# DeltaNet's 32-block forward substitution on VectorE instead of GpSimd

## The chip, the core and the metric

One core of one Trainium2 chip runs the whole program. The metric is device time in microseconds (us) for one execution. The engines are named as in the profile: PE (TensorE, matrix products), DVE (VectorE), ACT (ScalarE), POOL (GpSimd) and SP (SyncE, which issues most DMAs). Each takes its instructions in the order in which they stand in its own queue, and waits at the head of it until what the instruction needs is there.

## What is computed

The program is one decoder layer over 256 tokens of width 2048 in fp32: an input projection, three token mixers side by side (gated DeltaNet, Mamba-2 SSD, GLA), a merge, an MLP and a gated embedding. The change touches DeltaNet alone. Its reference, cut:

```python
m = jnp.where(strict, jnp.einsum('bnhik,bnhjk->bnhij', kb, k) * decay, 0.0)
a = m + jnp.eye(chunk, dtype=m.dtype)
u = lax.linalg.triangular_solve(a, v * beta[..., None], left_side=True, lower=True, unit_diagonal=True)
w = lax.linalg.triangular_solve(a, kb * jnp.exp(g)[..., None], left_side=True, lower=True, unit_diagonal=True)
```

The kernel works with chunks of 128 tokens, and solves with an explicit inverse T of the unit lower triangular matrix `a`. T is built from 32x32 diagonal blocks, each inverted by forward substitution; products on PE then join them to blocks of 64 and of 128.

## The kernel before

**Weights.** `weights` (L287 to L302) brings two k-tiles of a weight matrix at a time: one DMA from SP into a `raw` tile (512 KB for 512 columns, 344 KB for 344), a cast on ACT (L300) into `hi`, and a subtraction on DVE (L301, on record as L170, the line of the helper `tt`) into `lo`. PE then makes three products of each pair (hi with hi, lo with hi, hi with lo). There are four buffers each of `raw`, `hi` and `lo`. A fifth `hi` waits until PE has done with the first, a fifth `raw` until DVE has split the first. In what follows "the split lo_2263" is the subtraction that writes that tile; a chunk is the work of PE on one such tile.

**Mixers as background tasks.** The mixers run as generators (`Task`, `spawn`, `background`) between the projection's matmuls. A clock kept by the program, not by the chip, decides when a task goes a step further; a scheduler that knows priorities then puts the rows of each engine's queue in order. `feat_conv` makes a feature block of a mixer: products, DVE's copy out of PSUM (L170, with `r0bc`), twelve multiply-adds of a short convolution on DVE (L173, 128x256 each), a Silu on ACT (L457), and transposes on PE (L123) for whoever needs tokens on the partitions.

**DeltaNet.** `dn_task` runs twice, for four heads each (g = 0, 1: "group 0" and "group 1"). It makes M for two chunks of tokens, writes it to DRAM (L661), and reads it back with one 32x32 block for each of 32 partitions (L668). The 31 steps of the loop (L673 to L680) do the forward substitution there: step j multiplies a column of M with the rows of X that are done, and subtracts the product (two instructions, 31 to 256 elements on each partition, 5456 elements over the 31 steps for each of the two). L681 copies X transposed into XT. POOL then issues the DMAs that write both to DRAM (L682, L683), and four more that read them into tiles of 128 partitions, T and its transpose for either chunk of tokens (L688). PE's first use of T are 32x32 products, whose results ACT copies (L701) for the next products; ACT writes those into T (L716, L718), and stages of 64 and of 128 follow. The loop has the priority -LATER: in a queue it stands behind what else is ready.

Of the kernel before, what the change touches and what calls it, by code (L numbers as in the profile page):

```python
# [52 lines left out]
def tile_hybrid_block(ctx: ExitStack, tc: tile.TileContext, *args):  # L53
# [49 lines left out]
    def r3(ap, b):  # L103
        return ap.rearrange("p (a b) -> p a b", b=b)

    V, A, G = nc.vector, nc.scalar, nc.gpsimd
# [62 lines left out]
    def tt(eng, o, i0, i1, op):  # L169
        eng.tensor_tensor(out=o, in0=i0, in1=i1, op=op)  # L170
# [383 lines left out]
    def dr_blocks(d):  # L554
        return bass.AP(tensor=d.tensor, offset=d.offset, ap=[[HB // 4, 32], [P, 32], [1, 32]])
# [47 lines left out]
    def h4(tl):  # L603
        return lambda h: tl[:, h * P:(h + 1) * P]

    INV = G
    LATER = 1500

    def dn_task(g, qT, kT, vT):
# [63 lines left out]
        with tc.high_priority(-LATER):  # L673
            for j in range(31):
                n = 31 - j
                tmp = XT.rearrange("p a b -> p (a b)")[:, :n * (j + 1)]
                tmp = r3(tmp, j + 1)
                tt(INV, tmp, mb[:, j, j + 1:].unsqueeze(2).broadcast_to([32, n, j + 1]),
                   X[:, j, :j + 1].unsqueeze(1).broadcast_to([32, n, j + 1]), ALU.mult)
                tt(INV, X[:, j + 1:, :j + 1], X[:, j + 1:, :j + 1], tmp, ALU.subtract)  # L680
        INV.tensor_copy(out=XT, in_=X.rearrange("p i j -> p j i"))  # L681
        G.dma_start(out=dr_blocks(t_dr[0]), in_=X)  # L682
# [589 lines left out]
```

## Time and profile before

| | |
|---|---|
| runs shown | 1881.85, 1887.17, 1887.25 us (median 1887.17) |
| profiled execution | 1882.98 us |
| its span, first to last instruction | 1881.2 us |
| PE busy | 1846.9 us (98%) |
| DVE busy | 1161.0 us (62%) |
| POOL busy | 183.7 us (10%) |
| PE's granted clock, mean | 0.993 of full speed |
| the loop on POOL, group 0 | from 176.65 us, copy done at 230.74 |
| the loop on POOL, group 1 | from 313.66 us, copy done at 366.53 |

An engine's busy share is a mean over the span. Which engine is waited for at one place is read from what stands in brackets behind an instruction of the timeline: how long its engine idled before it, and what ended that.

### The profile page before, as it was taken

Reading aid. Unit: us, or ns where it says so; the run is one execution under the profiler, and the core shown is the slowest. Engines: PE = TensorE matmul, PEld = TensorE weight load, DVE = VectorE, ACT = ScalarE, POOL = GpSimd, SP = SyncE. Lnnn points to the kernel's source line nnn. Section 1 sums busy time; section 2 is a strip of 40 time slices with the busy share of each in tenths; the row PEclk is TensorE's granted clock in tenths of the full one; section 3 lists DMA queues with packets and bytes.
Section 4 is the critical chain, followed back from the end, with each engine's and each line's share of the span. In section 5 each row is a group of like instructions: output and inputs, shape, how many; then the busy total and the mean of one; then the engine's idle time right before and its main releaser. Section 6 shows DMA issues by size and latency. Waiting matters only on the chain.

```text
span 1881.2 us, 28343 instructions
## 1 busy us (share of the span) xinstructions
PE 1846.9 (98%) x11256; PEld 1659.0 (88%) x11256; DVE 1161.0 (62%) x1518; ACT 934.9 (50%) x1200; POOL 183.7 (10%) x243
## 2 busy tenths in 40 slices
PE   8999999899999999999999999999999999999997
PEld 8999989899888788888888898899889988998886
DVE  6567947878566666554565755455555555555675
ACT  6745564576455564454444644444433443444664
POOL 0004814800201220000000000000000000000001
PEclk9999989999999999999999999999999999999999
DMA  7765565465665546667676565666566566656563
GB/s 250 218 184 175 147 186 165 137 182 145 196 201 168 172 143 192 195 183 196 186 246 204 175 185 190 191 189 181 191 192 188 180 192 195 184 182 195 183 207 129
DMA packets 185573, 348.07 MB, mean 185 GB/s; under 512 B 14296, under 2 KB 33103, under 8 KB 184544
## 3 DMA queue, kind: packets, MB, share of 16 engines
q1 hardware_dynamic: 182992, 334.69, 58.8%
q0 software_dynamic: 2416, 11.56, 1.8%
q8 instruction: 88, 1.44, 0.3%
q14 instruction: 45, 0.37, 0.1%
q10 hardware_dynamic: 32, 0.01, 0.0%
HBM read 340.41 MB, written 5.80 MB: 184 GB/s over the span
## 4 chain that ended last, share of the span: by engine, by line
PE 69%; ACT 1%; POOL 1%; DVE 1%; issue 0%; DMA 0%; DVEq 0%; ACTq 0%
PE mm L114 67%; PE br L114 1%; PE br L123 1%; POOL b L170 1%; DVE lo L170 0%; ACT hi L300 0%; DMA raw<-in_w_in_dram 0%; DVE b L173 0%; ACT b L946 0%; ACT L1226 0%; ACT b L945 0%; ACT b L1114 0%; ACT L1236 0%; ACT b L1224 0%; DVE s L173 0%
## 5 line engine op out<-in xcount | busy, mean ns | idle before, releaser
L170 DVE TENSOR_TENSOR lo<-raw,hi 128x1024 fp32r<-128x1024 f32 (+2 forms) x644 | 771.7, 1202 | 621.9 <-ACT hi L300 618.5
L300 ACT CAST hi<-raw 128x1024 fp32r<-128x1024 f32 (+2 forms) x644 | 653.6, 1019 | 807.3 <-PE mm L114 702.3
L114 PE MATMUL mm<-ahi,hi 128*128 128x256 f32 x1728 | 492.2, 285 | 0.0
L114 PE MATMUL mm<-ahi,lo 128*128 128x256 f32 x1728 | 490.8, 284 | 0.0
L114 PE MATMUL mm<-alo,hi 128*128 128x256 f32 x1728 | 490.8, 284 | 0.0
L114 PE MATMUL mm<-hi,ahi 128*128 128x512 f32 (+2 forms) x992 | 372.0, 375 | 0.0
L114 PE MATMUL mm<-lo,ahi 128*128 128x512 f32 (+2 forms) x992 | 369.0, 372 | 2.8 <-DVE lo L170 1.6
L114 PE MATMUL mm<-hi,alo 128*128 128x512 f32 (+2 forms) x992 | 367.6, 371 | 0.0
L114 PEld LDWEIGHTS mm<-ahi,hi 128*128 128x128 f32 x1728 | 333.3, 193 | 0.5 <-ACT ahi L180 0.2
L114 PEld LDWEIGHTS mm<-alo,hi 128*128 128x128 f32 x1728 | 332.8, 193 | 0.8 <-issue 0.8
L114 PEld LDWEIGHTS mm<-ahi,lo 128*128 128x128 f32 x1728 | 333.3, 193 | 0.1
L114 PE MATMUL mm<-hi,m 128*128 128x512 f32 x1024 | 316.0, 389 | 0.0
L114 PEld LDWEIGHTS mm<-hi,m 128*128 128x128 f32 x1024 | 192.2, 188 | 39.9
L114 PEld LDWEIGHTS mm<-lo,ahi 128*128 128x128 f32 x992 | 187.2, 189 | 32.3 <-DVE lo L170 4.0
L114 PEld LDWEIGHTS mm<-hi,ahi 128*128 128x128 f32 x992 | 187.1, 189 | 28.0 <-issue 0.2
L114 PEld LDWEIGHTS mm<-hi,alo 128*128 128x128 f32 x992 | 187.1, 189 | 27.5
L114 PE MATMUL mm<-lo,m 128*128 128x512 f32 x512 | 199.2, 389 | 0.0
L114 PE MATMUL mm<-hi,b 128*128 128x512 f32 x416 | 134.1, 393 | 0.7 <-ACT hi L300 0.7
L114 PEld LDWEIGHTS mm<-lo,m 128*128 128x128 f32 x512 | 96.1, 188 | 19.7
L170 POOL TENSOR_TENSOR b<-b 128x128 f32<-128x128 f32 (+16 forms) x118 | 78.4, 679 | 162.0 <-ACT b L939 149.9
L114 PEld LDWEIGHTS mm<-hi,b 128*128 128x128 f32 x416 | 78.1, 188 | 17.0 <-ACT hi L300 1.1
L114 PE MATMUL mm<-lo,b 128*128 128x512 f32 x208 | 81.3, 391 | 0.8 <-DVE lo L170 0.8
(257 smaller groups left out, 1130.0 us busy)
## 6 DMA issues: line engine op xcount, KB each, us to landing
raw<-in_w_in_dram SPq DMA_DIRECT2D x200, 512.0 KB, 4.1
raw<-in_w_up_dram SPq DMA_DIRECT2D x128, 512.0 KB, 3.8
raw<-in_w_down_dram SPq DMA_DIRECT2D x128, 512.0 KB, 3.8
raw<-in_w_branch_dram SPq DMA_DIRECT2D x48, 512.0 KB, 4.6
raw<-in_w_in_dram SPq DMA_DIRECT2D x48, 344.0 KB, 3.5
raw<-in_w_out_dram SPq DMA_DIRECT2D x32, 512.0 KB, 4.8
raw<-in_w_ple_gate_dram SPq DMA_DIRECT2D x32, 512.0 KB, 4.5
raw<-in_w_in_dram SPq DMA_DIRECT2D x16, 352.0 KB, 3.4
```

Source lines behind the costliest of these rows:

```text
L114: nc.tensor.matmul(o, lhsT=lhsT, rhs=rhs, start=start, stop=stop, **kw)
L123: nc.tensor.transpose(o, i, ident)
L170: eng.tensor_tensor(out=o, in0=i0, in1=i1, op=op)
L300: A.copy(out=hi[:, :, :n], in_=raw[:, :, :n])
```

## The change

One name changes: the two tensor_tensor instructions of the loop and the copy L681 go to VectorE. Data, shapes, priority, and the DMAs that POOL issues stay.

```diff
-    INV = G
+    INV = V
     LATER = 1500
...
                 tt(INV, tmp, mb[:, j, j + 1:].unsqueeze(2).broadcast_to([32, n, j + 1]),
                    X[:, j, :j + 1].unsqueeze(1).broadcast_to([32, n, j + 1]), ALU.mult)
                 tt(INV, X[:, j + 1:, :j + 1], X[:, j + 1:, :j + 1], tmp, ALU.subtract)
         INV.tensor_copy(out=XT, in_=X.rearrange("p i j -> p j i"))
```

The scheduler puts the rows anew. DVE's queue has 62 instructions and a copy more for each group. Those of group 0 stand between the splits lo_2209 and lo_2820, those of group 1 between lo_3787 and lo_5033. This is the difference on DVE at the start of group 0; b_284 is X with M, b_285 the product:

```order
 L170 TENSOR_TENSOR lo_2209<-raw_2207,hi_2208 128x1024
+L170 TENSOR_TENSOR b_285_1942<-b_284_1941 32x31
+L170 TENSOR_TENSOR b_284_1941<-b_284_1941,b_285_1942 32x31
 L170 TENSOR_TENSOR lo_2263<-raw_2261,hi_2262 128x1024
+L170 TENSOR_TENSOR b_285_1942<-b_284_1941 32x60
+L170 TENSOR_TENSOR b_284_1941<-b_284_1941,b_285_1942 32x30x2
+L170 TENSOR_TENSOR b_285_1942<-b_284_1941 32x87
+L170 TENSOR_TENSOR b_284_1941<-b_284_1941,b_285_1942 32x29x3
+L170 TENSOR_TENSOR b_285_1942<-b_284_1941 32x112
+L170 TENSOR_TENSOR b_284_1941<-b_284_1941,b_285_1942 32x28x4
+L170 TENSOR_TENSOR b_285_1942<-b_284_1941 32x135
 L170 TENSOR_TENSOR lo_2293<-raw_2291,hi_2292 128x1024
```

Up to seven of them now stand between two splits. PE's queue is the same in the whole of group 0. In group 1 the copy stands as follows on DVE (b_515 is X, b_516 XT and then T):

```order
+L170 TENSOR_TENSOR b_516_3508<-b_515_3507 32x31
+L170 TENSOR_TENSOR b_515_3507<-b_515_3507,b_516_3508 32x31
 L170 TENSOR_TENSOR lo_5015<-raw_5013,hi_5014 128x2x344
+L681 COPY b_516_3508<-b_515_3507 32x1024
 L170 TENSOR_TENSOR lo_5033<-raw_5031,hi_5032 128x2x344
```

Before, POOL had made that copy at 366.53 us; the split that now stands behind it, lo_5033, ran at 406.28 us. PE's first products with group 1's T moved back by seven chunks, from the chunk of hi_4831 to that of hi_5068, where they now stand close to the products that need their results (b_686, b_687). PE's queue there, after:

```order
 L114 MATMUL mm_4879<-lo_5069,ahi_86 128x344
+L114 MATMUL br_4603<-b_516_3508,b_465_3206 32x32 x4
+L114 MATMUL br_4614<-b_516_3508,b_467_3214 32x32 x4
+L114 MATMUL br_4625<-c_651_4448,c_646_4427 128x64 x3
+L114 MATMUL br_4603<-b_516_3508,b_465_3206 32x32 x4
+L114 MATMUL br_4614<-b_516_3508,b_467_3214 32x32 x4
+L114 MATMUL br_4625<-c_651_4448,c_646_4427 128x64
+L114 MATMUL br_4625<-c_651_4448,c_648_4435 128x64 x4
+L114 MATMUL br_4637<-c_655_4457,bn_4455 128x512
+L114 MATMUL br_4669<-b_516_3508,b_686_4601 32x32 x4
```

Before, four chunks lay between br_4614 and br_4669. On ACT the copies L701 that lie between the two have also moved, behind two casts for the next projection, hi_5111 and hi_5141:

```order
+L300 CAST hi_5111<-raw_5110 128x1024
+L300 CAST hi_5141<-raw_5140 128x1024
+L701 COPY b_686_4601<-br_4603 32x128
+L701 COPY b_687_4602<-br_4614 32x128
+L701 COPY b_686_4601<-br_4603 32x128
+L701 COPY b_687_4602<-br_4614 32x128
```

Behind these places the queues meet the old order again; the last row of PE that differs belongs to group 1's final products, some 330 rows further on.

## Rows read from the trace of the kernel before

**Rows 1.** The page: busy time, share of the span, instructions.
```profile
PE 1846.9 (98%) x11256; PEld 1659.0 (88%) x11256; DVE 1161.0 (62%) x1518; ACT 934.9 (50%) x1200; POOL 183.7 (10%) x243
```

**Rows 2.** Busy us (instructions) by engine in three stretches, granted clock, DMA share.
```profile
120.00:177.00 57.00, 57.00 (x482) 57.00 (x481) 42.35 (x72) 28.03 (x35) 9.25 (x9) 1.00 0.61 178
177.00:231.00 54.00, 52.96 (x392) 52.38 (x391) 46.42 (x54) 28.58 (x42) 49.24 (x63) 1.00 0.55 153
...
314.00:367.00 53.00, 47.53 (x373) 46.80 (x372) 40.48 (x49) 25.29 (x34) 48.18 (x63) 0.97 0.47 135
```

**Rows 3.** Timeline of POOL: start, us, engine, line, op; the loop's ends.
```profile
176.65 0.23 POOL L170 TENSOR_TENSOR b<-b 32x31 f32<-32x31 f32 x1 [3.97 <-DMA b<-m_dr]
...
228.64 2.10 POOL L681 COPY b<-b 32x1024 f32<-32x1024 f32 x1
...
234.41 0.79 POOL L688 DMA_DIRECT2D b<-t_dr  x1 [2.13 <-DMA t_dr<-b]
```

**Rows 4.** Groups of DVE's instructions, 120 to 177 us: busy, mean ns.
```profile
L170 DVE TENSOR_TENSOR lo<-raw,hi 128x1024 fp32r<-128x1024 f32 x18 | 22.6, 1255 | 15.0 <-ACT hi L300 14.8
L173 DVE SCALAR_TENSOR_TENSOR b<-b,rowT,b 128x256 f32<-128x256 f32 x24 | 10.2, 479 | 0.0
...
L170 DVE TENSOR_TENSOR b<-br,s 128x512 f32<-128x512 f32 x3 | 2.0, 681 | 0.0
```

**Rows 5.** The same, 177 to 231 us, while POOL runs the loop.
```profile
L173 DVE SCALAR_TENSOR_TENSOR b<-b,rowT,b 128x256 f32<-128x256 f32 x24 | 17.6, 777 | 0.6 <-ACT b L452 0.6
L170 DVE TENSOR_TENSOR lo<-raw,hi 128x1024 fp32r<-128x1024 f32 x7 | 10.1, 1442 | 4.1 <-ACT hi L300 4.1
L170 DVE TENSOR_TENSOR lo<-raw,hi 128x704 fp32r<-128x704 f32 x8 | 9.9, 1246 | 0.6 <-ACT hi L300 0.6
...
L271 DVE TENSOR_SCALAR s<-s 128x32 f32<-128x32 f32 x1 | 1.9, 1948 | 0.7 <-ACT s L270 0.7
```

**Rows 6.** The same, 314 to 367 us, while POOL runs group 1's loop.
```profile
L173 DVE SCALAR_TENSOR_TENSOR b<-b,rowT,b 128x256 f32<-128x256 f32 x19 | 14.7, 813 | 0.1
...
L170 DVE TENSOR_TENSOR cbm<-br,cst 128x128 f32<-128x128 f32 x2 | 0.6, 284 | 1.2 <-PE br L114 1.2
```

**Rows 7.** Timeline of DVE: two short instructions, each needing the one before.
```profile
292.88 0.17 DVE L170 TENSOR_TENSOR s<-s 128x8 f32<-128x8 f32 x1
293.08 0.37 DVE L173 SCALAR_TENSOR_TENSOR s<-s,s 128x8 f32<-128x8 f32 x2
```

**Rows 8.** Groups of DVE's instructions, whole span: one that reads with a stride.
```profile
L968 DVE TENSOR_REDUCE ga<-c 128x128 f32<-128x512 f32 x8 | 8.4, 1056 | 0.0
```

**Rows 9.** PE's waits, 165 to 525 us: us, times, longest.
```profile
PE br L123 <- ACT b L457: 5.5, 1, 5.5
...
PE mm L114 <- DVE b L437: 0.9, 1, 0.9
```

**Rows 10.** Timeline of PE at the first products with group 0's T.
```profile
242.21 0.69 PE L114 MATMUL br<-b,b 32*32 32x32 f32 x16
...
243.57 0.32 PE L114 MATMUL mm<-lo,ahi 128*128 128x344 f32 x1
243.72 0.32 PE L114 MATMUL mm<-hi,alo 128*128 128x344 f32 x1
246.66 0.53 PE L114 MATMUL br<-b,b 32*32 32x32 f32 x6 [2.62 <-ACT b L701]
```

**Rows 11.** DMA issues of 225 to 260 us: KB each, us to landing.
```profile
b<-t_dr POOLq DMA_DIRECT2D x4, 256.0 KB, 6.5
```

**Rows 12.** Timeline of ACT before PE's wait at 345 us.
```profile
343.87 1.06 ACT L457 ACTIVATE b<-b 128x1024 f32<-128x1024 f32 x1 [5.39 <-DVE b L173]
```

**Rows 13.** Stretches after PE's waits: busy us by engine, granted clock.
```profile
246.00:256.00 10.00, 9.34 (x76) 7.73 (x77) 2.53 (x6) 5.07 (x13) 0.00 (x0) 0.51 0.70 193
346.00:348.00 2.00, 2.00 (x11) 2.00 (x11) 1.44 (x4) 0.85 (x2) 1.84 (x3) 0.51 0.67 175
```

**Rows 14.** Timeline of PE at the first products with group 1's T.
```profile
398.73 0.69 PE L114 MATMUL br<-b,b 32*32 32x32 f32 x16
```

## Prediction

> **What bounds the kernel now.** The page's first part says that PE is busy for 1846.9 us, 98% of the span [rows 1]. So the end moves only when PE waits less or more, or runs at another clock. The next view is the table of windows: POOL's loops fill the stretches 177 to 231 and 314 to 367 us, and PE has 1.0 us of idle time in the first and 5.5 in the second [rows 2]. That 5.5 us is all that the profile offers for removal while the loop runs. POOL itself is not waited for there: its loop of group 0 runs from 176.65 us to 230.74 (the copy's end) [rows 3], that of group 1 ends at 366.53, and PE's first products with T come at 242.21 [rows 10] and 398.73 us [rows 14]. The change can then act in three ways: POOL's quiet may speed up DVE, DVE's added work may make splits late for PE, and T may come too late.
>
> **What DVE gets rid of.** The groups of DVE's instructions in the stretch before the loop, compared with the same groups during it, show the price of POOL's company. A multiply-add of the convolutions (128x256) takes 479 ns while POOL is nearly quiet [rows 4], 777 ns in group 0's loop [rows 5], and 813 in group 1's [rows 6]. A 1024-wide split takes 1255 against 1442 ns.
>
> The Trainium skill (page "SBUF — State Buffer", section "Who interferes with whom") says that DVE's second pair of SBUF ports is shared with GpSimd, as an exclusive lock. The trace agrees for instructions with two SBUF operands (479 against 777 ns), and by that rule a quiet POOL would give the difference back.
>
> In group 0 the excess is 24 x 0.298 = 7.2 us for the multiply-adds, 7 x 0.187 = 1.3 for the wide splits, 8 x 0.36 = 2.9 for the 704-wide splits (1246 ns against 0.88 by the line below), and 1.8 for L271, together 13.2 us. In group 1 the multiply-adds alone have 19 x 0.334 = 6.3 us.
>
> **What DVE gets.** A tensor_tensor takes 284 ns for 128 elements [rows 6] and 681 for 512, one of whose operands is broadcast as in the loop [rows 4]; the line through them is 0.15 us + 1.04 ns for an element. The loop is a chain, each instruction needing the one before; such a pair stands at 292.88 + 0.17 = 293.05 and 293.08 us, a gap of 0.03 to 0.04 [rows 7]. So one costs 0.186 us + 1.04 ns an element: 62 x 0.186 = 11.5, plus 10912 x 1.04 ns = 11.35, together 22.9 us. The copy reads with a stride of 32 words. If that is free it costs 0.15 + 1.07 = 1.2 us; if it is like the strided read of L968 (512 elements in 1056 ns, 1.77 ns each [rows 8]) it costs 2.0. I take 1.9, since the stride is what the two share. That makes 24.8 us a group, against 54.1 on POOL. A price of 1.77 ns for every element of the loop is the upper bound: 10912 x 0.73 ns = 8 us more.
>
> [...]
>
> **Group 0.** DVE is busy for 46.4 of 54 us [rows 2]. With the change that is 46.4 - 13.2 + 24.8 = 58.0 us from about 176.6 on, if it never idles: the copy ends at 233.4 (laid out row by row in the new order, where neighbours overlap by some hundredths) to 234.6. I take 233.7, that is 3 us later than POOL's. T then takes its old way: 3.7 us from the copy's end to the first read's issue (234.41 [rows 3]) and 6.5 us for a read [rows 11], that is 240.9 before, for a use at 242.21. The slack is 1.3 us, so PE waits about 1.7 us more. POOL's other rows here are memsets and the DMA L529, which now stands among T's reads instead of behind them, so it is issued about when it was. Splits: a late one made PE wait 0.9 us before (it is put down to L437, the row behind it) [rows 9]; laying out the new queue gives waits of 0.2, 0.6 and 1.0 us at lo_2762, lo_2780 and lo_2820, some 0.9 more, in which T comes nearer too, since PE is later for it. I put group 0 at +1.5 us, with bounds of -2 and +10 (the latter with the 8 us above).
>
> **Group 1, the start.** Here lies PE's longest wait, 5.5 us for the Silu of L457 [rows 9]. ACT idled 5.39 us before that Silu, until DVE's last multiply-add [rows 12]. Twelve of them precede it; without POOL each takes 0.334 us less, 4.0 us together, of which 0.3 goes to an instruction of the loop that now stands between them: 3.7 us less wait. The clock: after the wait it was granted at 0.51 in 346 to 348 us, the lower level of 1.2 GHz [rows 13], while the stretch with the wait of 0.9 us kept 1.00 [rows 2, 9]. If the wait shrinks to 1.7 us most of that half speed goes too, 1.2 us (of 2 to 3 us at half). Sum -4.9, between 0 and -7. Some two thirds of the loop's 24.8 us, 17 us, stand in the stretch up to 367 us, where DVE has 53 - 40.5 = 12.5 us idle [rows 2] and gets 6.3 back: it fits, just. The rest stands behind, up to 400 us; there PE reads a split some us after it is made, and none is late in my layout.
>
> **Group 1, the end.** The copy ends at about 398 us by the layout (before: 366.53). By the same 3.7 and 6.5 us T lands at about 408. PE's first products with it were at 398.73 us [rows 14]; they are now seven chunks later, each of 12 products at 0.155 us [rows 10], and the start's gain is taken off: 398.7 + 13 - 4.9 = 406.8. So the first of the four reads may be there in time, and the last has no slack. The products that follow need ACT's copies L701, which now stand behind hi_5141 and so behind a raw DMA that runs together with T's reads. In group 0 the same pattern made PE wait 2.62 us [rows 10], and the clock from 246 to 256 us had a mean of 0.51 [rows 13]. In the new place some 4 us of other small products lie between; I take +1 us, between 0 and +6.
>
> **Sum.** +1.5 - 4.9 + 1.0 = -2.4 us. The profiled execution took 1882.98 us (span 1881.2 and 1.8 around it), so 1880.6 us. It lies 4.2 us below the median of the runs shown and near the fastest; runs of one kernel differ by 5 us here, and 0.3% (5.6 us) is about what a measurement tells from no change.
>
> **The rivals.**
> *A larger gain.* The move of T's reads by 3 us may take them off the raw DMA that held ACT in group 0. Then the wait of 2.62 us [rows 10] and most of the 10 us near half clock [rows 13], some 3.5 of at most 5 us of PE's time, go as well, and group 1's new wait does not come: -2.4 - 1 - 2.6 - 3.5 = -9.5, 1873.5 us. For it: POOL's whole disturbance ends. Against it: T's reads and the weight reads still meet, only later.
> *A wait in a new place.* Group 1's T or its L701 comes late as in group 0: PE waits 2.6 us or more and loses 3.5 at half clock: -2.4 - 1 + 6 = +2.6, 1885.6 us. For it: the new order on ACT. Against it: the small products between.
> *DVE becomes the bound (slower).* The loop's operands, rows of 1 to 31 elements on 32 partitions, cost 1.77 ns an element. Then group 0's copy ends at 242 us and T comes 8 us later still, and in group 1 the copy ends some 6 us later, against no slack: -2.4 + 8 + 6 = +11.6, 1894.6 us, and more with half clock. The point from which it decides is about 1.3 ns an element (2.8 us more in each group). Against it: the broadcast operand in rows 4 runs at 1.04 ns.
> *The contention stays.* If something other than POOL slows DVE in these stretches, DVE has 46.4 + 24.8 = 71 us of work in 54, T is 17 us late in group 0, and it is 1897 us or more. Against it: the stretch before has the same instructions at 479 ns.
>
> **How the numbers follow.** The forecast has 0.42 (own range 1877 to 1884), the larger gain 0.28, the wait in a new place 0.17, DVE as the bound 0.09, the contention 0.04. Faster by over 0.3% holds most of the larger gain (0.25) and the forecast's lower edge (0.05): 0.30. Slower holds the last two and a quarter of the new wait: 0.17; the rest, 0.53, is within 0.3%. The range leaves out the end of the larger gain and of the last two: 1870 to 1893.
>
> **What would show it.** Right: the multiply-adds at 0.48 us in both stretches; the loop's 256-element instructions at about 0.42 us; group 0's copy at 1.9 us, ending near 233.7; PE's wait for L457 at 1 to 2.5 us; half clock gone after it. Wrong: multiply-adds still near 0.8; loop instructions above 0.5; PE's waits for splits beyond 3 us in 177 to 235; waits at T's first products beyond 4 us; group 1's L701 at the head of PE's waits.

## The result, and the profile after

The changed kernel took 1868.6 us (median of 4 executions, 1867.83 to 1870.28), beside 1884.5 us for the kernel before: a ratio of 0.9919, with a 95% interval from 0.9903 to 0.9936. In two later comparisons on other occasions the same kernel gave 0.9932 [0.9914, 0.9950] and 0.9939 [0.9919, 0.9958]. By these ratios the gain is some 11 to 15 us (the medians of the three comparisons lie 15.9, 11.5 and 8.8 us apart). The forecast was 2.4 us.

The profiled execution took 1870.28 us, 12.7 less than that of before. The page's busy times and two rows of the windows (busy us by engine, then granted clock and DMA share) answer to [rows 1, 2]:

```profile
PE 1840.2 (98%) x11256; PEld 1653.3 (88%) x11256; DVE 1172.0 (63%) x1644; ACT 930.6 (50%) x1197; POOL 88.8 (5%) x117
```

```profile
177.00:231.00 54.00, 54.00 (x404) 54.00 (x403) 51.81 (x121) 28.81 (x42) 0.00 (x0) 1.00 0.58 157
314.00:367.00 53.00, 52.55 (x409) 51.77 (x408) 51.12 (x109) 29.44 (x40) 0.00 (x0) 1.00 0.54 153
```

POOL is quiet in both stretches, DVE is busy for 51.8 of 54 and 51.1 of 53 us, and PE's idle time falls from 1.0 to nothing and from 5.5 to 0.45 us. The groups of DVE's instructions in the first stretch (busy us, mean ns) answer to [rows 4, 5]:

```profile
L173 DVE SCALAR_TENSOR_TENSOR b<-b,rowT,b 128x256 f32<-128x256 f32 x24 | 10.2, 467 | 0.0
L170 DVE TENSOR_TENSOR lo<-raw,hi 128x1024 fp32r<-128x1024 f32 x8 | 9.6, 1206 | 0.0
L170 DVE TENSOR_TENSOR lo<-raw,hi 128x704 fp32r<-128x704 f32 x8 | 7.0, 873 | 0.0
```

The multiply-adds are at 467 ns, where they had 777. The wide split is at 1206 ns: the 1255 of [rows 4], which I had taken for the quiet price, still had some of POOL's company in it (one of its 18 took 1.79 us, while POOL worked at 150 to 156 us). DVE's timeline shows the loop and the copy (start, us):

```profile
204.98 0.41 DVE L170 TENSOR_TENSOR b<-b 32x255 f32<-32x255 f32 x1
205.43 0.41 DVE L170 TENSOR_TENSOR b<-b,b 32x255 f32<-32x255 f32 x1
...
231.09 1.00 DVE L681 COPY b<-b 32x1024 f32<-32x1024 f32 x1
```

An instruction of 255 elements takes 0.41 us and the next starts 0.45 us after it, as forecast (0.186 + 255 x 1.04 ns = 0.45). The copy takes 1.00 us (1.17 in group 1), not 1.9. PE's waits from 165 to 525 us, the start of its products with group 0's T, and the Silu before group 1's transposes answer to [rows 9, 10, 12]:

```profile
PE br L114 <- DVE b L170: 1.8, 1, 1.8
PE br L114 <- ACT b L718: 1.7, 1, 1.7
...
PE br L114 <- DMA b<-t_dr: 0.5, 1, 0.5
PE br L123 <- ACT b L457: 0.5, 1, 0.5
```

```profile
243.25 0.66 PE L114 MATMUL br<-b,b 32*32 32x32 f32 x16 [0.52 <-DMA b<-t_dr]
...
244.98 0.43 PE L114 MATMUL br<-b,b 32*32 32x32 f32 x8
...
251.46 0.43 PE L114 MATMUL br<-b,b 32*32 32x32 f32 x8 [1.74 <-ACT b L718]
```

```profile
335.26 1.06 ACT L457 ACTIVATE b<-b 128x1024 f32<-128x1024 f32 x1 [0.60 <-DVE b L173]
```

The wait of 5.5 us for L457 is down to 0.5, and ACT idles 0.60 us before that Silu instead of 5.39. The wait of 2.62 us for L701 is gone; a new one of 1.74 us for L718 stands a stage further on. The clock, in windows that answer to [rows 13], with one more at group 1's products with T:

```profile
246.00:256.00 10.00, 8.26 (x95) 7.31 (x92) 4.28 (x11) 4.73 (x13) 0.00 (x0) 0.91 0.70 221
346.00:348.00 2.00, 2.00 (x19) 2.00 (x19) 1.90 (x5) 0.78 (x1) 0.00 (x0) 1.00 0.67 179
400.00:414.00 14.00, 14.00 (x158) 12.34 (x157) 9.80 (x11) 10.09 (x19) 0.00 (x0) 1.00 0.48 160
```

The stretch from 246 to 256 us has a clock of 0.91, where it had 0.51; what is left of the lower level there begins at 254 us, behind the wait for L718:

```profile
254.00:258.00 4.00, 4.00 (x23) 3.63 (x22) 1.04 (x5) 0.96 (x2) 0.00 (x0) 0.57 0.80 248
```

Adding up two-microsecond windows between 120 and 520 us that were granted less than 0.9, PE's lost time is 8.5 us before and 1.7 after.

To see where the 12.7 us came from, PE's first product with each `lo` tile was set beside the same product of before. The program's start was 1.3 us later in this execution; against that, PE gained 1.2 us at 221 us (the wait put down to L437), lost 1.1 up to 243, gained 4.7 by 252 and gave 1.6 back by 260 (the L718 wait), gained 1.7 around 300, 6.5 between 306 and 348, and 1.0 at 376 to 380. Another 1.3 us came at 1050 us, far from the loops, where the kernel before ran some 3 us at the lower level and this execution did not:

```profile
1047.00:1051.00 4.00, 3.68 (x17) 3.45 (x18) 3.67 (x8) 2.64 (x7) 0.00 (x0) 0.59 0.78 299
```

The row is that of before. Of the profiles of the other kernels eight have this stretch too and the rest do not; nothing ties it to the change.

### The profile page after: what moved, and what is told of

Same layout as the page of the kernel before. It is cut to its first block, busy times and chain, and to the rows that moved or that the text cites. A ratio compares the mean times of both kernels' runs of the same rounds, so it can differ in the third digit from the quotient of the medians.

```text
span 1868.5 us, 28352 instructions
## 1 busy us (share of the span) xinstructions
PE 1840.2 (98%) x11256; PEld 1653.3 (88%) x11256; DVE 1172.0 (63%) x1644; ACT 930.6 (50%) x1197; POOL 88.8 (5%) x117
## 4 chain that ended last, share of the span: by engine, by line
PE 69%; ACT 1%; POOL 1%; DVE 1%; issue 0%; DVEq 0%; ACTq 0%
PE mm L114 67%; PE br L114 1%; POOL b L170 1%; PE br L123 1%; ACT hi L300 0%; DVE lo L170 0%; DVE b L173 0%; ACT b L945 0%; ACT b L946 0%; ACT L1226 0%; ACT b L1114 0%; ACT L1236 0%; ACT b L1224 0%; DVE s L173 0%; ACT b L939 0%
## 5 line engine op out<-in xcount | busy, mean ns | idle before, releaser
L170 DVE TENSOR_TENSOR b<-b,b 32x31 f32<-32x31 f32 (+10 forms) x88 | 45.5, 521 | 15.4 <-ACT b L946 14.0
```

## The experiments

Ratios are to the kernel before, run on the same chip in the same session; the changed kernel's own are 0.9919, 0.9932 and 0.9939.

**Which group.** `g0_only` and `g1_only` move one group's loop each.

```diff
-    INV = G
     def dn_task(g, qT, kT, vT):
         hs = slice(g * 4, g * 4 + 4)
+        INV = V if g == 0 else G        # g0_only;  g == 1 in g1_only
```

> Group 0's loop on VectorE, group 1's on GpSimd. My theory: the gain is GpSimd's quiet, stretch by stretch, so the two groups add up. From PE's times at the same splits, group 0 has about 5 of the 13 us (the start of the program, which was 1.3 us later in that execution, taken off): 1877 to 1881 us in a run beside 1884, with the 2.6 us wait for L701 gone, and group 1's wait for L457 of 5.5 us still there. Rival: the gain hangs on the new order of PE, ACT and SP that comes with group 1, and group 0 alone gives nothing: within 2 us of the kernel before, or slower by the late T that I forecast (+1.5 us).

> Group 1's loop on VectorE, group 0's on GpSimd; PE's order is that of the changed kernel. My theory: about 8 of the 13 us, 1874 to 1878 us, the wait for L457 below 1 us with full clock after it, and group 0's waits of 0.9 and 2.6 us as before. Rival (order): if the order of PE makes the gain, all of it comes here, 1868 to 1871 us.

Measured: g0_only 0.9977 [0.9964, 0.9990], 1881.6 us; g1_only 0.9938 [0.9919, 0.9956], 1875.2 us. The gains, 0.23% and 0.62%, add up to 0.85%, beside the changed kernel's 0.81, 0.68 and 0.61; each is known to within 0.13 to 0.2, so this fits two gains that add up and does not prove it. That the order alone makes it is out: g0_only has PE's old order, row by row, and still gains (so has loop_out below, which gains most). PE's waits in the two profiles, g0_only first:

```profile
PE br L123 <- ACT b L457: 5.4, 1, 5.4
PE br L114 <- DMA b<-t_dr: 1.6, 1, 1.6
```

```profile
PE br L114 <- ACT b L701: 2.1, 1, 2.1
...
PE br L123 <- ACT b L457: 0.5, 1, 0.5
```

Group 1 loses its Silu wait and keeps group 0's L701; group 0 the other way about, but with 1.6 us for T's reads in place of L701. In that profile the clock from 246 to 256 us is 0.53, as before: of group 0's forecast loss by a late T this execution has the whole.

**Is it POOL's company?** `loop_out` takes the loop away from both engines; `pool_busy` is the changed kernel with a second chain of the same sizes on POOL; `pool_memset` fills POOL's time with writes alone.

```diff
-            for j in range(31):
+            for j in range(1):          # loop_out, pool_memset (INV = G)
...
+            tt(G, dsc[:, :n], dsc[:, 256:256 + n], dsc[:, 256:256 + n], ALU.mult)      # pool_busy, 31 times
+            tt(G, dsc[:, 256:256 + n], dsc[:, 256:256 + n], dsc[:, :n], ALU.subtract)
...
+            for _ in range(55):                                                        # pool_memset
+                G.memset(XT.rearrange("p a b -> p (a b)"), 0.0)
```

> Leaves out 30 of the 31 steps of both loops; the rest stays on GpSimd, so T is there some 50 us earlier and neither engine has the work. My theory: the multiply-adds take 0.48 us in both stretches, and the gain is that of the changed kernel or a little more, 12 to 17 us (1867 to 1872 us). If the added work on VectorE itself cost much, this kernel is faster than the changed one by more than 5 us. Rival (order): no gain in the stretches where the order does not change, under 5 us in all.

> The changed kernel with a second chain on GpSimd, of the same 62 instruction sizes, on a scratch tile that nobody reads, started by the same read of M. My theory: the multiply-adds are back at 0.75 to 0.85 us, the loop's instructions on VectorE are longer too, T is late, and the kernel is slower than the one before, 1888 to 1900 us. Rival (order): GpSimd's company costs VectorE time but not the kernel, within 4 us of the changed kernel's 1869.

> Leaves out 30 of the 31 steps in both groups, as loop_out, and GpSimd fills the time with 55 memsets of 32x1024 (writes alone, about 54 us) before T goes out. If any GpSimd access to SBUF slows VectorE, the multiply-adds take 0.7 us or more and the time is that of the kernel before, within 4 us. If it takes a read by GpSimd, they take 0.48 us, and the time is 1866 to 1872 us with T as late as before.

Measured: loop_out 0.9893 [0.9876, 0.9909], 1866.3 us; pool_busy 1.0069 [1.0053, 1.0086], 1898.9 us. So the loop on VectorE costs some 2 to 8 us more than no loop at all (medians of different sessions; in loop_out T is there earlier as well), and POOL's company takes the whole gain and more. DVE's groups in pool_busy between 177 and 231 us, and PE's waits:

```profile
L173 DVE SCALAR_TENSOR_TENSOR b<-b,rowT,b 128x256 f32<-128x256 f32 x24 | 14.5, 646 | 0.0
L170 DVE TENSOR_TENSOR lo<-raw,hi 128x1024 fp32r<-128x1024 f32 x8 | 9.6, 1206 | 0.0
...
L170 DVE TENSOR_TENSOR b<-b 32x256 f32<-32x256 f32 x1 | 0.8, 794 | 0.0
```

```profile
PE br L123 <- ACT b L457: 11.1, 1, 11.1
PE mm L114 <- DVE lo L170: 9.4, 9, 2.3
```

The multiply-adds are at 646 ns (less than the 750 to 850 that I expected), the loop's own 256-element instructions at 0.79 and 0.78 us instead of 0.41, and PE waits 11.1 us for the Silu. In pool_memset the first two rows are DVE's multiply-adds and a short tensor_scalar, the third is POOL's timeline, the fourth PE's wait, the fifth the window behind it:

```profile
L173 DVE SCALAR_TENSOR_TENSOR b<-b,rowT,b 128x256 f32<-128x256 f32 x24 | 10.4, 477 | 0.7 <-ACT b L452 0.6
...
L273 DVE TENSOR_SCALAR s<-s 128x32 f32<-128x32 f32 x1 | 0.7, 678 | 0.0
```

```profile
179.01 48.03 POOL L676 MEMSET b<- 32x1024 f32 x48
```

```profile
PE br L114 <- DMA b<-t_dr: 3.2, 1, 3.2
```

```profile
246.00:264.00 18.00, 17.17 (x128) 14.36 (x128) 2.63 (x6) 6.59 (x16) 0.00 (x0) 0.54 0.60 194
```

POOL writes for 48 us at a stretch and the multiply-adds stay at 477 ns: it is reads by POOL that slow them, not writes. (Not everything on DVE is untouched: L273 took 0.68 us and L268, of the same shape, 0.47, against 0.17 and 0.16 in the changed kernel.) Yet its one execution took 1885.28 us, as long as the kernel before. The memsets held T back (the last ended at 235.0 us), PE waited 3.2 us for T's reads and then ran at 0.54 of its clock for 18 us. Here my expectation, that a quiet DVE would give 1866 to 1872 us, failed. In this execution the late T cost as much as the quiet DVE gave.

**Why did group 0's L701 wait go?** In the kernel before, ACT stood 3.72 us for a weight read, with the copies L701 behind it in its queue; the 344 KB weight reads took longest to land there (issues of 225 to 260 us: before, after, and t_early, which follows):

```profile
245.57 0.76 ACT L300 CAST hi<-raw 128x688 fp32r<-128x688 f32 x1 [3.72 <-DMA raw<-in_w_in_dram]
```

```profile
raw<-in_w_in_dram SPq DMA_DIRECT2D x9, 344.0 KB, 7.2
```

```profile
raw<-in_w_in_dram SPq DMA_DIRECT2D x9, 344.0 KB, 5.7
```

```profile
raw<-in_w_in_dram SPq DMA_DIRECT2D x11, 344.0 KB, 3.5
```

In the changed kernel the weight reads of 212 to 240 us were issued 0.4 to 4.0 us sooner than before (the start taken off), and T's first read at about the same distance from PE as before (7.1 us ahead of it, 7.8 before). My reading is that the splits, which free the buffers, were no longer late. Two tests: `split_late` makes splits late again, `t_early` leaves the splits slow and sends T out sooner, by leaving out group 0's last five steps.

```diff
+        if g == 0:                                   # split_late: behind the copy L681
+            for _ in range(4):
+                V.tensor_copy(out=dsv.rearrange("p (i j) -> p i j", j=32), in_=X[:, :, :16].rearrange("p i j -> p j i"))
...
-            for j in range(31):
+            for j in range(31 if g else 26):         # t_early, with INV = G
```

> The changed kernel, with four useless copies (32x512) on VectorE right behind group 0's copy of X, before and between the next splits; nobody reads them, and T's DMAs don't wait for them. Theory: in the kernel before, group 0's wait for L701 came from splits that were late, which gave the raw buffers back late, so that the weight reads met T's reads. Then splits that are 1 to 2 us late here bring back a wait of ACT for a raw DMA of 2 to 4 us at 240 to 246 us and a wait of PE of 2 us or more with half clock: 3 to 7 us slower than the changed kernel (1872 to 1876). Rival: that wait went for another reason (when T's reads were issued), and the copies cost under 1.5 us.

> The kernel before, GpSimd doing the loop; group 0's last 5 steps are left out, so T is there about 5 us earlier, at the same company of GpSimd until then. Theory: T's reads no longer meet the weight reads that ACT needs before L701; the wait of 2.6 us and the half clock after it go, 4 to 7 us faster than the kernel before (1877 to 1881), though the multiply-adds still take 0.77 us and group 1's wait for L457 stays. Rival (VectorE's late splits made that wait): it stays, and the time is within 2 us of the kernel before.

split_late: 0.9938 [0.9924, 0.9953], 1872.5 us, some 4 us slower than the changed kernel's first result, but no slower than its two later ones. The time came out in the range, but by another way than I expected:

```profile
PE br L114 <- DVE adt L170: 3.6, 1, 3.6
```

The copies delayed the small instructions that make `adt`, and PE stood 3.6 us there, before the weight reads could meet T's. So this run does not decide. t_early: 0.9979 [0.9970, 0.9988], 1878.7 us, some 4 us faster than the kernel before, the low end of what I expected. DVE's multiply-adds and PE's waits in it:

```profile
L173 DVE SCALAR_TENSOR_TENSOR b<-b,rowT,b 128x256 f32<-128x256 f32 x24 | 17.6, 776 | 0.6 <-ACT b L452 0.6
```

```profile
PE br L123 <- ACT b L457: 5.4, 1, 5.4
PE mm L114 <- DVE lo L170: 1.2, 2, 0.9
```

The multiply-adds are as slow as before, and the Silu's wait is there; what is gone is the wait at group 0's T, and with it the stretch at half clock. The weight reads went out no sooner than before, so it was T's that moved (228.88 instead of 234.41 us). So group 0's loss goes with how T's reads lie to the weight reads. It is shown for T moved; that the weight reads' move did it in the changed kernel fits the trace, but no run isolates it.

**Does the late T cost by its wait, or by the clock?**

```diff
+        if g == 0:                                   # t_late
+            for _ in range(2):
+                G.tensor_copy(out=dsm, in_=XT[:, :16, :].rearrange("p a b -> p (a b)"))
         G.dma_start(out=dr_blocks(t_dr[1]), in_=XT)
```

> The changed kernel, in group 0 with two useless copies (32x512) on GpSimd after the loop, so that T's reads go out some 2 us later; nothing else changes. In the profiles so far, PE at half clock for 8 to 10 us goes with a wait of 1.6 us or more at the 32x32 products with T, and waits of 1.2 us or less there go without. Theory: the wait for T's reads at about 243 us grows from 0.5 us to 2 us or more, the clock falls to the lower level for 8 to 10 us, and the kernel is 4 to 8 us slower than the changed one (1872 to 1877). Rival: a late T costs the wait alone, 1 to 2.5 us.

> The changed kernel unaltered, for more executions. In nearly all kernels so far the time of an execution goes with its mean granted clock: 1867 to 1870 us at 0.997 to 0.998, 1874 to 1877 at 0.993 to 0.995, above 1880 at 0.989 to 0.990. The changed kernel's four executions all had 0.997 or 0.998. If its gain is real in full, ten more stay at 1867 to 1872 us. If four of four was chance (the stages with small products of T at half clock in some executions, as in g1_only, mask_on_v and t_late, all with its order of PE), a third or more of them have 0.995 or less and 1874 us or more, and the median rises to 1870 to 1875.

> The changed kernel unaltered, on the same chip as g0_sooner, for the comparison: 1867 to 1870 us in about two of three executions and 1873 to 1876 in the others.

t_late: 0.9949 [0.9932, 0.9965], 1874.2 us (1867.15 to 1882.86). Its copies moved the first read hardly at all and the last three by about 0.8 us, so it is a weak test of its theory: PE's wait for T's reads in its profile is 1.3 us, not the 2 or more that I expected, and 20 us at half clock follow it all the same. But its ten executions fall into groups, and so do the changed kernel's (every execution of the three comparisons, with its mean granted clock):

```
changed, clock 0.997-0.998 (8): 1867.8 1868.2 1868.5 1868.5 1868.7 1868.8 1869.9 1870.3
changed, clock 0.992-0.995 (6): 1872.2 1873.5 1874.5 1875.2 1876.1 1876.4
t_late,  clock 0.997-0.998 (4): 1867.2 1867.8 1868.3 1870.0
t_late,  clock 0.989-0.995 (6): 1873.8 1874.6 1875.3 1875.7 1876.4 1882.9
before,  beside t_late: all 21 at 0.991 to 0.994, 1880.4 to 1887.0
```

A clock lower by 0.004 over 1870 us is 7 us, which is the distance between the groups. The profile of after_again has its stretch at group 1's products with T, that of after_third at group 0's:

```profile
398.94 0.66 PE L114 MATMUL br<-b,b 32*32 32x32 f32 x16 [0.62 <-DMA b<-t_dr]
```

```profile
400.00:414.00 14.00, 14.00 (x102) 11.46 (x102) 7.66 (x8) 6.91 (x13) 0.00 (x0) 0.53 0.32 105
```

```profile
PE br L114 <- DMA b<-t_dr: 1.4, 1, 1.4
```

```profile
246.00:256.00 10.00, 10.00 (x83) 8.27 (x81) 2.74 (x7) 4.13 (x11) 0.00 (x0) 0.50 0.59 192
```

In the changed kernel's first profile the window 400 to 414 us had 1.00 and 158 products; here it has 0.53 and 102. So four of four good executions were luck; by their mean clocks eight of fourteen are without a long stretch of this kind (the first profile, one of the eight, has the 3 us at 254), and of the 81 executions of the kernel before that stand beside the experiments not one had a mean clock above 0.994. The expectation for after_third (two of three at 1867 to 1870) missed: one of four was.

**Group 1's new place.** Three kernels change where group 1's products or the loop's rows stand, and one takes L529 from POOL.

```diff
-        yield 2.0
+        yield 6.0 if g else 2.0                      # spread: between the first and the second products with T
-        with tc.high_priority(-LATER):
+        with tc.high_priority(-(LATER if g == 0 else 500)):    # later_500;  LATER = 0 for both in later_0
-            G.dma_start(out=Gd, in_=rows_[:NT * n])
+            nc.scalar.dma_start(out=Gd, in_=rows_[:NT * n])    # gate_on_act
```

> The changed kernel, but group 1's task pauses longer between its first products with T and the next (yield 6.0 for 2.0), so that on PE some chunks of weight products stand between them again. Theory: half clock at 404 to 416 us, seen in four profiles with the close order, comes from small products that stand close together; spread, it does not come, and the executions have no mean clock under 0.995 unless group 0 has its stretch: median 1867 to 1871. Rival: the closeness has no part in it: clocks and times as the changed kernel's, or worse where later stages meet.

> The changed kernel with LATER = 500 for group 1 alone: its copy stands 12 rows earlier on VectorE and T's first products some 40 rows earlier on PE. If the new, late place of group 1's products is what costs in some executions, this has fewer of them: 1867 to 1871 us. If all of the loop that stands ahead of other work delays splits and the convolution, as later_0 did, it is 2 to 8 us slower than the changed kernel.

> The changed kernel with LATER = 0: the loop stands in VectorE's queue without being put behind other work, so T is earlier in group 1, and more of the loop stands ahead of the splits and multiply-adds. Theory (the work on VectorE is free only where it fills gaps): splits and the Silu of L457 come late, PE waits for them, 2 to 8 us slower than the changed kernel. Rival (the late T is what still costs): 1 to 3 us faster, since the wait at group 1's first products cannot come.

> The changed kernel, with the small DMA of the gate sums (L529) issued by ACT instead of GpSimd, where it stands among T's reads. PE's order is the same. Theory: the gate's rows come back 2 us earlier, VectorE (idle for 5.6 us before L538) and ACT go on earlier, PE's wait of 1.7 us for L718 goes: 1 to 3 us faster than the changed kernel. Rival: the gate's DMA is late because of T's and the weight reads themselves, and nothing changes (within 1 us).

Measured: spread 0.9957 [0.9943, 0.9972], later_500 0.9945 [0.9925, 0.9965], later_0 0.9980 [0.9967, 0.9992], gate_on_act 0.9958 [0.9944, 0.9971]. None is better than the changed kernel. In spread, PE's second products with group 1's T stand 16 us behind the first, and its profile has its half clock at group 0's T (244 to 254 us) and 3 us of it at 422. Its theory, that closeness brings the stretch, is not confirmed: no execution of it had more than 0.995. later_500 took 1873.6 us, between its two expectations, and decides nothing. later_0, at 1880.5 us, is slower than I expected: PE waits 1.2 us for the Silu and 2.4 us for another product of DVE's that cost the changed kernel nothing, and although T is earlier its profile has 10 us at half clock at 404 us. gate_on_act was to save 1 to 3 us and saved nothing: its profile has no wait for L718, but neither has that of after_third, which is the changed kernel, and it has a half-clock stretch at both places.

At group 1's new place the stretch also comes with no wait ahead of it. In g1_only PE idles nowhere between 380 and 420 us, and yet:

```profile
404.00:416.00 12.00, 12.00 (x86) 9.59 (x86) 7.66 (x8) 6.75 (x13) 0.00 (x0) 0.57 0.34 107
```

The same holds for t_late (410 to 416 us at 0.50) and later_0 (404 to 410 us at 0.50); in gate_on_act a wait of 0.2 us stands there. A late T is not needed for it.

**The masks on DVE too.**

```diff
-            tt(G, r3(Eb, P), r3(E, P), bc4(cc[:, c * 4:c * 4 + 4]), ALU.mult)
-            tt(G, r3(E, P), r3(E, P), mbc(LE), ALU.mult)
+            tt(V, r3(Eb, P), r3(E, P), bc4(cc[:, c * 4:c * 4 + 4]), ALU.mult)
+            tt(V, r3(E, P), r3(E, P), mbc(LE), ALU.mult)
```

> The changed kernel, with the two masks of E (four multiplies of 128x512 a group) on VectorE as well, so that GpSimd has only DMAs and memsets before 480 us. If GpSimd's company is what costs, the splits at 151 to 157 and 295 to 302 us are shorter, and PE's wait of 1.8 us at 297.85 for VectorE's product with E goes: 1 to 4 us faster than the changed kernel. Rival: VectorE has no room for 2.8 us more in a group, or the wait is for another part of the chain: within 1 us of it, or slower.

Measured: 0.9985 [0.9972, 0.9997], 1880.7 us, with executions up to 1888 at 0.988. The last of POOL's company goes and some 9 to 12 us of the gain with it: its profile shows 3.2 us of waits for T's reads (1.2 us in group 0, 2.0 in group 1) and half clock from 404 to 418 us. PE's wait for the product with E shrank to 1.2 us and did not go.

**T of group 0 sooner.**

```diff
-        with tc.high_priority(-LATER):
+        with tc.high_priority(-(0 if g == 0 else LATER)):
```

> The changed kernel with LATER = 0 for group 0 alone: PE's order is the same, and on VectorE group 0's copy stands ahead of three more splits, so T's reads go out some 4 to 5 us sooner. Theory: group 0's waits for T and for L718 (0.5 and 1.7 us in the changed kernel's profile) and its chance of half clock go, and what is left of the disturbed executions is group 1's: 1865 to 1869 us in most, median 0 to 4 us faster than the changed kernel. Rival: the loop ahead of splits makes these late, and PE's waits for splits before 235 us take the gain away: 1869 to 1873 us.

Measured: 0.9925 [0.9912, 0.9937], 1869.3 us (1867.20 to 1872.04), against 0.9939 and 1874.2 us for the changed kernel on the same chip (after_third). POOL's issue of T's first read and PE's waits:

```profile
227.65 0.77 POOL L688 DMA_DIRECT2D b<-t_dr  x1 [1.80 <-DMA t_dr<-b]
```

```profile
PE br L114 <- DVE b L170: 1.8, 1, 1.8
PE br L114 <- ACT b L718: 1.5, 1, 1.5
```

The read goes out 7 us sooner than in after_third (234.99), no wait for T is left, and no execution is above 1872.1. The wait for L718 stays (1.5 us), and a half-clock stretch of 10 us follows it in the profile. The intervals overlap, and the changed kernel's first ratio was 0.9919, so that it beats the changed kernel is not shown.

## Why the prediction was wrong

**What held.** POOL's company was the price of DVE's multiply-adds: they went to 467 ns, came back with a second chain, and stayed at 477 beside writes. The wait for L457 is down to 0.4 or 0.5 us in all three profiles of the changed kernel. A loop instruction costs 0.186 us + 1.04 ns an element; that DVE becomes the bound by a price of 1.77 ns is out, and so is a contention that stays. The place of the largest single gain, the Silu of L457, was right.

**Group 1, the start: mis-sized.** I gave it -4.9 us; it measured -6.5. The step that was short is the Silu's wait, "3.7 us less": the twelve multiply-adds before it gave 4.7 us (9.76 to 5.05) where I had 4.0, and I did not count the two splits between them, which gave 0.9 (before, then after):

```profile
334.96 1.70 DVE L170 TENSOR_TENSOR lo<-raw,hi 128x1024 fp32r<-128x1024 f32 x1
...
339.81 1.65 DVE L170 TENSOR_TENSOR lo<-raw,hi 128x1024 fp32r<-128x1024 f32 x1
```

```profile
329.77 1.21 DVE L170 TENSOR_TENSOR lo<-raw,hi 128x1024 fp32r<-128x1024 f32 x1
...
332.49 1.21 DVE L170 TENSOR_TENSOR lo<-raw,hi 128x1024 fp32r<-128x1024 f32 x1
```

The wait shrank by 5.0 us; the clock behind it gave 1.5 instead of 1.2.

**Group 0: wrong in sign.** The step "the copy ends 3 us later than POOL's" failed: it ended at 232.09 in an execution that was 1.3 us late from its start, so at the same time as POOL's. The copy took 1.00 us where I chose 1.9 of a bound from 1.2 to 2.0, the quiet splits were cheaper than the row that I had taken as quiet, and I left the six 688-wide splits out of the excess (998 to 859 ns, 0.8 us). The choice of 1.9 rested on one form of L968; the same view has a second, also with a stride, at 1.07 ns an element:

```profile
L968 DVE TENSOR_REDUCE ga<-c 128x128 f32<-128x256 f32 x8 | 3.4, 423 | 0.0
```

So T was late by 0.5 to 1.5 us at PE instead of 1.7.

**The larger omission** is that I left group 0's wait of 2.62 us and its 10 us at half clock where they were, as if they belonged to the kernel, and put their going into a rival with 0.28 (-9.5 us). The mean clocks of the kernel before (0.994 or less in all 81 executions) fit such a stretch in every one, though only one of them was profiled; in eight of fourteen of the changed kernel's they leave no room for a long one. So the rival's result came in these, by another way than it said: T's reads did not move by 3 us, the weight reads went out sooner. In the profiled execution PE gained 3.2 us net between 217 and 260 us where I forecast a loss of 1.5. Of the 11.6 us that the forecast lacks in the profiled execution (14.0 with the late start taken off, against 2.4), 4.7 are here, 1.6 at the Silu, 1.7 around 300 us, 1.0 at 376 (a wait for DVE that went), 1.0 at group 1's end, where the forecast loss did not come, and 1.3 at 1050 us; 0.3 are spread over the rest. The number 0.51 for 246 to 256 us stood in [rows 13], and the wait that led to it was one of 2.6 us on a transfer that the change moves against others. Of the clock I priced only what stood behind the Silu, and by looking for what could go "while the loop runs" I looked past the stretches behind it. Luck does not explain the miss: the changed kernel's six slower executions are still 7 to 11 us below the median of before.

**Group 1, the end.** The layout was wrong: the copy ended at 390.94 us, not at about 398, the first read went out 1.9 us after it, not 3.7, and PE's first products stood at 400.73, not 406.8:

```profile
389.77 1.17 DVE L681 COPY b<-b 32x1024 f32<-32x1024 f32 x1
```

```profile
392.87 0.77 POOL L688 DMA_DIRECT2D b<-t_dr  x1 [0.85 <-DMA t_dr<-b]
```

```profile
400.73 0.69 PE L114 MATMUL br<-b,b 32*32 32x32 f32 x16
```

So PE did not wait there. "T with no slack" was right as a danger all the same: of the changed kernel's three profiles one has a wait of 0.6 us for T's reads there, with 14 us at half clock behind it, and two have no wait. The +1 us lies between executions that have nothing there and some that lose 7 us (half of the 14). That L701, behind hi_5141, would make PE wait at this place came in no profile.

**Around 300 us** 1.7 us came that I had not looked for: the wait for DVE's product there (1.96 us before, 1.80 after) was followed by half clock before and not after. loop_out, later_0 and later_500 have the stretch again after a wait of 1.9 us, and after_again has a wait of 2.0 us without it. None of the changed kernel's three profiles has it; whether that is the change or chance no run shows.

**Open.** What decides in an execution whether the clock falls at the products with T. At group 0's, a wait of 1.6 us or more was followed by it in every profile; with 0.5 to 1.5 us some have it (gate_on_act, t_late, after_third; g0_sooner at L718) and some do not (the changed kernel's first, up to the wait for L718, after_again, mask_on_v). At group 1's new place it has come with a wait of 2.0 us, of 0.6, and with none.

## What to carry to other kernels

Before pricing a move to another engine by its own time, read what that engine's company costs the others: the same instruction's mean in a stretch where the neighbour is quiet and in one where it works. Then list every stretch at half clock, with the wait ahead of it if there is one, and ask of each whether the change moves one of the two things that met there. In the kernel before such a stretch cost some 5 us behind a wait of 2.6; over the profiles it lasted from 3 to 20 us, and it came in some executions of one kernel and not in others. Where the gain is of that size, look at ten executions and their mean clock, not at one profile.

## What the runs showed of the hardware

- Reads by POOL slow DVE's instructions with two SBUF operands (467 to 777 ns for 128x256); memsets by POOL do not (477 ns beside 48 us of them). The Trainium skill (page "SBUF — State Buffer", section "Who interferes with whom") says just that: a DVE instruction with two SBUF inputs contends with a GpSimd instruction that reads SBUF, not with one that only writes it. The trace agrees (777 and 477 ns).
- In pool_busy the wide splits stayed at 1206 ns while the multiply-adds went to 646, with no idle time of DVE before either; in the kernel before the splits suffered too (1442). I have no explanation that a run supports.
- A tensor_copy that reads with a stride of 32 words took 1.00 and 1.17 us for 1024 elements, no more than the 0.15 + 1.07 of the line for a tensor_tensor; a contiguous copy of this size stands in no run. The Trainium skill (page "Vector Engine (DVE) Microarchitecture Reference", section "The SBUF access granule: adjacent pairs") has 1.73 ns a column, against 1.054, where one of two sources hops at every element. This copy, with one source, took about 1 ns an element; for it the measurement decides.
- The clock at the products with T stayed at the lower level for 7 to 20 us at a time in most profiles that have it, and for 3 us in some (the changed kernel's first). At the waits of 300 and 345 us it was 3 us in the kernel before; at the wait for L457 it was 7 us in g0_only and t_early, and 10 us in pool_busy.
